# Ten of eleven groups of an up projection by Strassen's seven block products, in a decoder layer on Trainium2

## The chip, the core and the metric

The kernel runs on one core of a Trainium2 chip. The metric is the device time of one execution in microseconds, the median of several runs.

## What is computed

One decoder layer for 512 tokens of width 1024, all in fp32: a mixer of four parallel heads groups, a cross attention into 256 memory tokens, and a gated feed-forward part with a causal depthwise convolution over three tokens. The change lies in the feed-forward part:

```python
def rms_norm(t, g):
    y = t * lax.rsqrt(jnp.mean(t * t, axis=-1, keepdims=True) + RMS_EPS)
    return y * g

def conv_ffn(xn, w_up, w_conv, w_down):          # xn (512, 1024), w_up (1024, 5632), w_down (2816, 1024)
    u = causal_depthwise_conv(xn @ w_up, w_conv)  # over three tokens, each column by itself
    a, g = jnp.split(u, 2, axis=-1)
    return (a * jax.nn.silu(g)) @ w_down

h = h + conv_ffn(rms_norm(h, g_ffn), w_up, w_ffconv, w_down)
return rms_norm(h, g_final)
```

## The kernel before

Precision first. Every fp32 operand of a matmul is split into two parts of 12 bits each, hi and lo: ScalarE writes hi (a cast), VectorE lo (operand minus hi). A product is then three matmuls, hi x hi, hi x lo and lo x hi (`mm3`, L153 to L156), added up in PSUM. Weights come in loads of 512 KB, [128, 1024] values, on SyncE's DMA queue, into one of 3 raw buffers, and their parts into one of 4 buffers each (`Weights`, L97; `load_split` splits at L119 and L120). Activations are kept feature-major, [128 features, 512 tokens], as hi and lo (`Parts`, filled at L150 and L151).

The feed-forward part begins when the residual h2 is written (`Project`, L764): VectorE adds the old residual (L781), `fill` makes the parts, times the gain of the norm, ScalarE squares (L787) and GpSimd adds the squares (L788). The norm's factor per token is found after the first matmuls have begun (`h2.norm`, L792) and spread over the partitions by matmuls as `rb` [128, 512] (`row_broadcast`, L282); it is applied to what comes out of the up projection.

The up projection (L960 to L974) has 11 groups. A group is 256 columns of the a half and the same 256 of the g half, each by `pair_gemm` (L180): two output tiles [128, 512] in PSUM, 8 chunks of 128 features, three matmuls for each, so 48 matmuls of a moving operand 128x512, and 96 per group. `conv3` (L916) takes each output tile: times rb (VectorE, L918), the tap of the token itself (ScalarE, L920), and the two earlier tokens (VectorE, L921 and L922). ScalarE applies silu to g (L933) and GpSimd multiplies by a (L938 for the first ten tiles, L943 for the twelve later). The result au is split (`split_au`, L910), the first ten tiles at once, the others after the stage (L975). Between the halves of the first groups, TensorE turns the residual to token-major (`h2_tokens`, L949, copied by ScalarE at L958), and it stays in SBUF for the end.

The down projection (L1010 to L1035) is token-major: two halves of 512 output columns, four blocks of 128 tokens, 24 matmuls for each load of weights; the last block of the second half is done in two pieces of 256 columns. The final norm follows (`finish`, `scale_out`).

Each engine does its instructions in the order of the program, as a scheduler has settled it from the code's order and priorities; buffers of a pool (28 of [128, 1024] for activations, 18 of [128, 512] for others) are handed out in turn and waited for.

Of the kernel before, what the change touches and what calls it, by code (L numbers as in the profile page):

```python
# [1061 lines left out]
```

## Time and profile before

| | us |
|---|---|
| median of 3 runs | 753.76 (753.26 to 754.99) |
| span of the profiled execution | 752.2 |
| TensorE busy in it | 742.5 (99%), 3809 matmuls and transposes |
| TensorE's weight loads | 620.8 (83%), beside the matmuls |
| VectorE busy | 428.6 (57%) |
| ScalarE busy | 339.4 (45%) |
| GpSimd busy | 127.8 (17%) |

The profile is that of one execution; what the runs' clock sees and the span doesn't, 1.5 us, is about the same for each. Busy shares are means over stages. The up projection runs from about 370 to 615 us and the down projection from there to the end.

### The profile page before, as it was taken

To read this page: it belongs to the slowest core of one execution; us is meant where nothing else is said; L and a number is where in the kernel's file an instruction comes from. 1 tells how busy PE (TensorE), PEld (TensorE's weight loads), DVE (VectorE), ACT (ScalarE), POOL (GpSimd) and SP (SyncE) were. 2 spreads that over 40 slices of the span, in tenths; PEclk is the share of its full clock that TensorE was granted. 3 is DMA by queue.
4 is the path that set the end of the run, shared out by engine and by line. 5 is a ranking of instruction groups with operands and counts; after the bars stand their busy time and mean duration, and the time that the engine had idled before them with its cause. 6 is when DMAs were issued, how large, how long until landed. Compare 5 with 4: busy or idle time off the path is not lost.

```text
span 752.2 us, 9886 instructions
## 1 busy us (share of the span) xinstructions
PE 742.5 (99%) x3809; PEld 620.8 (83%) x3809; DVE 428.6 (57%) x723; ACT 339.4 (45%) x581; POOL 127.8 (17%) x140
## 2 busy tenths in 40 slices
PE   8999999999999999999999999999999999999996
PEld 7898877899988888888888888888888888888885
DVE  4868576768635436546546656666565567323214
ACT  4773654678634434444335334343333335213214
POOL 5233040033303300001211110111100114003000
PEclk9999999999999999999999999999999999999998
DMA  9743512233434422102322232232332322423202
GB/s 297 228 131 107 169 58 83 85 114 113 147 120 126 139 86 85 56 29 65 104 84 85 85 112 85 92 99 90 103 94 90 107 84 85 140 86 111 85 0 112
DMA packets 67711, 78.37 MB, mean 104 GB/s; under 512 B 3038, under 2 KB 58886, under 8 KB 67664
## 3 DMA queue, kind: packets, MB, share of 16 engines
q1 hardware_dynamic: 65040, 71.33, 30.5%
q0 software_dynamic: 2032, 5.36, 2.2%
q10 hardware_dynamic: 592, 1.05, 0.4%
q8 instruction: 30, 0.49, 0.3%
q14 instruction: 17, 0.14, 0.1%
HBM read 73.46 MB, written 4.27 MB: 103 GB/s over the span
## 4 chain that ended last, share of the span: by engine, by line
PE 98%; DMA 1%; ACT 0%; DVE 0%; issue 0%; SPq 0%; ACTq 0%
PE p_upg L154 5%; PE p_upg L156 5%; PE p_upg L155 5%; PE p_upa L154 5%; PE p_upa L155 5%; PE p_upa L156 5%; PE p_dn L154 5%; PE p_dn L156 5%; PE p_dn L155 5%; PE p_h L155 4%; PE p_h L154 4%; PE p_h L156 4%; PE p_xq L154 2%; PE p_xq L155 2%; PE p_xq L156 2%; PE p_xv L217 1%
## 5 line engine op out<-in xcount | busy, mean ns | idle before, releaser
L154 PE MATMUL p_upg<-h2g_hi,whi_upg 128*128 128x512 f32 x176 | 70.0, 398 | 0.0
L156 PE MATMUL p_upg<-h2g_hi,wlo_upg 128*128 128x512 f32 x176 | 69.5, 395 | 0.0
L155 PE MATMUL p_upg<-h2g_lo,whi_upg 128*128 128x512 f32 x176 | 69.5, 395 | 0.0
L154 PE MATMUL p_upa<-h2g_hi,whi_upa 128*128 128x512 f32 x176 | 69.2, 393 | 0.0
L155 PE MATMUL p_upa<-h2g_lo,whi_upa 128*128 128x512 f32 x176 | 68.9, 391 | 0.0
L156 PE MATMUL p_upa<-h2g_hi,wlo_upa 128*128 128x512 f32 x176 | 68.6, 390 | 0.0
L154 PE MATMUL p_dn<-whi_dn,au_hi 128*128 128x512 f32 (+1 forms) x176 | 66.7, 379 | 0.0
L156 PE MATMUL p_dn<-whi_dn,au_lo 128*128 128x512 f32 (+1 forms) x176 | 66.7, 379 | 0.0
L155 PE MATMUL p_dn<-wlo_dn,au_hi 128*128 128x512 f32 (+1 forms) x176 | 66.5, 378 | 0.0
L120 DVE TENSOR_TENSOR wlo_dn<-raw_dn,whi_dn 128x1024 fp32r<-128x1024 f32 x22 | 27.6, 1256 | 59.1 <-ACT whi_dn L119 59.0
L119 ACT CAST whi_upg<-raw_upg 128x1024 fp32r<-128x1024 f32 x22 | 23.1, 1049 | 79.3 <-PE p_upg L155 66.0
L119 ACT CAST whi_dn<-raw_dn 128x1024 fp32r<-128x1024 f32 x22 | 23.1, 1049 | 72.4 <-PE p_dn L156 30.2
L788 POOL TENSOR_TENSOR acc_h<-acc_h,sq_h 128x512 f32<-128x512 f32 x14 | 21.8, 1559 | 150.2 <-ACT sq_h L787 150.0
L943 POOL TENSOR_TENSOR au<-uo_a,sg 128x512 f32<-128x512 f32 x12 | 23.2, 1938 | 116.1 <-ACT sg L933 116.1
L120 DVE TENSOR_TENSOR wlo_upg<-raw_upg,whi_upg 128x1024 fp32r<-128x1024 f32 x22 | 27.0, 1225 | 23.2 <-ACT whi_upg L119 23.2
L156 PEld LDWEIGHTS p_upg<-h2g_hi,wlo_upg 128*128 128x128 f32 x176 | 33.1, 188 | 7.9
L154 PEld LDWEIGHTS p_upg<-h2g_hi,whi_upg 128*128 128x128 f32 x176 | 33.1, 188 | 7.7
L155 PEld LDWEIGHTS p_upg<-h2g_lo,whi_upg 128*128 128x128 f32 x176 | 33.1, 188 | 7.6
L156 PEld LDWEIGHTS p_upa<-h2g_hi,wlo_upa 128*128 128x128 f32 x176 | 33.0, 188 | 7.3
L154 PEld LDWEIGHTS p_upa<-h2g_hi,whi_upa 128*128 128x128 f32 x176 | 33.1, 188 | 7.1
L155 PEld LDWEIGHTS p_upa<-h2g_lo,whi_upa 128*128 128x128 f32 x176 | 33.1, 188 | 6.8
L156 PEld LDWEIGHTS p_dn<-whi_dn,au_lo 128*128 128x128 f32 x176 | 33.0, 188 | 6.7
(407 smaller groups left out, 1944.2 us busy)
## 6 DMA issues: line engine op xcount, KB each, us to landing
raw_upa<-in_w_up_dram SPq DMA_DIRECT2D x22, 512.0 KB, 3.6
raw_upg<-in_w_up_dram SPq DMA_DIRECT2D x22, 512.0 KB, 3.5
raw_dn<-in_w_down_dram SPq DMA_DIRECT2D x22, 512.0 KB, 3.8
raw_xk<-in_w_xkv_dram SPq DMA_DIRECT2D x8, 512.0 KB, 3.4
raw_xv<-in_w_xkv_dram SPq DMA_DIRECT2D x8, 512.0 KB, 3.6
raw_h<-in_w_out_dram SPq DMA_DIRECT2D x8, 512.0 KB, 3.5
raw_xq<-in_w_xq_dram SPq DMA_DIRECT2D x8, 512.0 KB, 3.5
raw_h<-in_w_xo_dram SPq DMA_DIRECT2D x8, 512.0 KB, 3.4
```

Of the source, the lines that this page charges most:

```text
L119: nc.scalar.copy(self.hi[:, ks], self.raw[:, ks])
L120: nc.vector.tensor_tensor(self.lo[:, ks], self.raw[:, ks], f(self.hi[:, ks]), op=ALU.subtract)
L154: nc.tensor.matmul(psum, ah, bh, start=first, stop=False, skip_group_check=True)
L155: nc.tensor.matmul(psum, ah, bl, start=False, stop=False, skip_group_check=True)
L156: nc.tensor.matmul(psum, al, bh, start=False, stop=last, skip_group_check=True)
L217: nc.tensor.matmul(p_[b], parts.hi[k][:, t], hi[:, kk, :], start=k == 0 and b % per == 0, stop=False, skip_group_check=per > 1)
L788: nc.gpsimd.tensor_tensor(acc, acc, sq, op=ALU.add)
L943: nc.gpsimd.tensor_tensor(au[i][:, j, :], ff.pop(("a", c)), sg, op=ALU.mult)
```

## The change

The first group of the up projection stays. For the other ten the product of a group is taken as one of 2 x 2 blocks: the weights as (features 0 to 511, 512 to 1023) x (256 columns of a, 256 columns of g), the activations as two halves of the features x two halves of the tokens. In place of eight products of blocks there are seven (q1 to q7, after Winograd's form), each [512 features, 256 columns] x [512 features, 256 tokens]: 4 chunks x 2 tiles x 3 matmuls = 24 matmuls of a moving operand 128x256, 168 per group. Line numbers from here on are those of the changed kernel.

- The activations' side is made once, in `operands` (L972): the residual is normed in place on VectorE (L985), GpSimd makes sums and differences (L989), and seven operands are split into parts (L981, L982; two of the lo parts on GpSimd).
- The weights' side is made per group (`Blocks`, L1011): five plain loads of 512 KB on SyncE's queue, and two of these tiles have another block of weights added to them by an adding DMA from GpSimd's queue (L1025): s3 and s1. GpSimd adds two further pairs, x11 += s1 and x12 += x11 (L1059, L1064), 128x1024 each. `product` (L1034) splits each of the seven.
- The outputs (`strassen`, L1047): al, be and ga are PSUM banks [128, 512], with the tokens' halves and tiles side by side. Products add up in al and be, and between them ScalarE copies al to SBUF (c1, c2, c3) and VectorE and ScalarE put the four output tiles ua, ug together by halves. `conv3` then works as before, without the multiplication by rb; silu is done in place.
- On TensorE the order is q1, q2, q6, q7, q5 of group 1, then q1 of group 2, q3 and q4 of group 1, q2, q6, q7 and q5 of group 2, and so on: q3 and q4 of a group stand between q1 and q2 of the next.
- All splits of au of groups 1 to 10 come after the up stage. The residual, token-major, is spilled to DRAM by GpSimd's DMAs (L963) and loaded again for the end; its transposes are moved, one half into the last part of the projection to h2, one half into group 0.
- There are 7 raw buffers instead of 3, 3 split buffers instead of 4 (for hi and lo each), 26 and 17 buffers instead of 28 and 18. In `Project` the square stands before the fill.

The core of the diff:

```diff
+ACTS, TMPS, RAWS, SPLITS = 26, 17, 7, 3
...
-    def conv3(p_, t, name):
-        u = tmp(f"u_{name}")
-        nc.vector.tensor_tensor(u, p_, ff["rb"], op=ALU.mult)
+    def conv3(u, t, name):
         o = tmp(f"uo_{name}")
...
+        def load(name, g, k, add=None):
+            t = raw_tile(f"{name}_{i}")[:, :1024]
+            v = t.rearrange("p (k n) -> p k n", n=256)
+            nc.sync.dma_start(v, src(g, k))
+            if add:
+                nc.gpsimd.dma_start(v, src(*add), accum_op=ALU.add)
+            return t
+        self.x11 = load("x11", 0, 0)
+        self.s3 = load("s3", 1, 0, (0, 0))
+        self.s1 = load("s1", 1, 0, (1, 1))
+        self.x12 = load("x12", 0, 1)
+        self.x22 = load("x22", 1, 1)
+
+    def product(psum, w, y_, name, fresh):
+        hi, lo = (t[:, :1024] for t in part_tiles(name))
+        nc.scalar.copy(hi, w)
+        nc.vector.tensor_tensor(lo, w, f(hi), op=ALU.subtract)
+        hi, lo = (t.rearrange("p (k n) -> p k n", n=256) for t in (hi, lo))
+        for k in range(4):
+            for j in range(2):
+                cs = slice(j * P, (j + 1) * P)
+                mm3(psum[:, j * 256 : j * 256 + 256], hi[:, k, cs], lo[:, k, cs], y_hi[y_][:, k, :], y_lo[y_][:, k, :], fresh and k == 0 and j == 0, k == 3)
+
+    def strassen(i):
+        w = blocks.pop(i)
+        al, be, ga = ps(f"p_al{i}"), ps(f"p_be{i}"), ps(f"p_ga{i}", "sc")
+        ua, ug = [tmp(f"ua{i}{j}") for j in range(2)], [tmp(f"ug{i}{j}") for j in range(2)]
+        product(al, w.x11, Y11, f"q1_{i}", True)
+        c1 = tmp(f"c1_{i}")
+        nc.scalar.copy(c1, al)
+        yield
+        product(ga, w.x12, Y21, f"q2_{i}", True)
+        for j, t in enumerate(tiles):
+            nc.vector.scalar_tensor_tensor(ua[j][:, :256], ga[:, t], -1.0, c1[:, t], op0=ALU.mult, op1=ALU.subtract)
+        nc.gpsimd.tensor_tensor(w.x11, w.x11, w.s1, op=ALU.add)
+        yield
+        product(al, w.x11, T2, f"q6_{i}", False)
+        c2 = tmp(f"c2_{i}")
+        nc.scalar.copy(c2, al)
+        nc.gpsimd.tensor_tensor(w.x12, w.x12, w.x11, op=ALU.add)
+        yield
+        product(be, w.s3, T3, f"q7_{i}", True)
+        yield
+        product(al, w.s1, T1, f"q5_{i}", False)
+        c3 = tmp(f"c3_{i}")
+        nc.scalar.copy(c3, al)
+        for j, t in enumerate(tiles):
+            nc.vector.tensor_tensor(ug[j][:, 256:], c3[:, t], be[:, t], op=ALU.subtract)
+        if i + 1 < NJ // 2:
+            blocks[i + 1] = Blocks(i + 1)
+        yield
+        product(al, w.x12, Y22, f"q3_{i}", False)
+        for j, t in enumerate(tiles):
+            nc.scalar.activation(ua[j][:, 256:], al[:, t], AF.Copy, scale=-1.0)
+        a = [conv3(ua[j], 2 * i + j, f"a{2 * i + j}") for j in range(2)]
+        yield
+        product(be, w.x22, T4, f"q4_{i}", False)
+        for j, t in enumerate(tiles):
+            nc.vector.tensor_tensor(ug[j][:, :256], c2[:, t], be[:, t], op=ALU.subtract)
+        for j in range(2):
+            gate(2 * i + j, a[j], ug[j])
...
+    for i in range(2, NJ // 2):
+        now = strassen(i)
+        pump(now, 1)
+        pump(before, 99)
+        pump(now, 4)
+        before = now
```

In the rows of the orders below a name is the program's, with the number of its instance behind it: whi_q7_6 is the hi part of the weights of q7 of group 6, uo_g10 the convolved g of tile 10 (group 5).

VectorE in the steady part, changed kernel, from the end of group 5's convolutions of a:

```order
L924 SCALAR_TENSOR_TENSOR uo_a11_5426<-ua51_5107,fcw_2913,uo_a11_5426 128x510
L1083 TENSOR_TENSOR ug50_5108<-c2_5_5280,p_be5_5104 128x256
L1083 TENSOR_TENSOR ug51_5109<-c2_5_5280,p_be5_5104 128x256
L1038 TENSOR_TENSOR wlo_q7_6_5536<-raw_s3_6_5345,whi_q7_6_5535 128x1024
L923 SCALAR_TENSOR_TENSOR uo_g10_5460<-ug50_5108,fcw_2913,uo_g10_5460 128x511
L923 SCALAR_TENSOR_TENSOR uo_g11_5467<-ug51_5109,fcw_2913,uo_g11_5467 128x511
L924 SCALAR_TENSOR_TENSOR uo_g10_5460<-ug50_5108,fcw_2913,uo_g10_5460 128x510
L924 SCALAR_TENSOR_TENSOR uo_g11_5467<-ug51_5109,fcw_2913,uo_g11_5467 128x510
L1058 SCALAR_TENSOR_TENSOR ua60_5358<-p_ga6_5357,c1_6_5390 128x256
L1058 SCALAR_TENSOR_TENSOR ua61_5359<-p_ga6_5357,c1_6_5390 128x256
L1038 TENSOR_TENSOR wlo_q5_6_5564<-raw_s1_6_5348,whi_q5_6_5563 128x1024
```

VectorE before, from the outputs of the g half of group 4:

```order
L918 TENSOR_TENSOR u_g8_4713<-p_upg40_4651,rb_h2_3969 128x512
L120 TENSOR_TENSOR wlo_upg5_1_4847<-raw_upg5_1_4845,whi_upg5_1_4846 128x1024
L921 SCALAR_TENSOR_TENSOR uo_g8_4715<-u_g8_4713,fcw_2913,uo_g8_4715 128x511
L922 SCALAR_TENSOR_TENSOR uo_g8_4715<-u_g8_4713,fcw_2913,uo_g8_4715 128x510
L918 TENSOR_TENSOR u_g9_4727<-p_upg41_4652,rb_h2_3969 128x512
L912 TENSOR_TENSOR au_lo4_4722<-prod8_4723,au_hi4_4721 128x512
L921 SCALAR_TENSOR_TENSOR uo_g9_4729<-u_g9_4727,fcw_2913,uo_g9_4729 128x511
L922 SCALAR_TENSOR_TENSOR uo_g9_4729<-u_g9_4727,fcw_2913,uo_g9_4729 128x510
L120 TENSOR_TENSOR wlo_upa6_0_4898<-raw_upa6_0_4896,whi_upa6_0_4897 128x1024
L912 TENSOR_TENSOR au_lo4_4722<-prod9_4735,au_hi4_4721 128x512
L918 TENSOR_TENSOR u_a10_4801<-p_upa50_4739,rb_h2_3969 128x512
```

Where a group had two operations on each PSUM tile and four weight parts, the conv steps and assemblies of group 5 now stand between the weight parts of q7 and q5 of group 6, which TensorE takes up next.

GpSimd at the entry of the stage, changed kernel (h12 and h13 hold the features 512 to 1023 of the residual; ylo2 and ylo6 are the lo parts of Y22 and T4; the L1025 row is an adding DMA):

```order
L1064 TENSOR_TENSOR raw_x12_1_4014<-raw_x12_1_4014,raw_x11_1_4006 128x1024
L989 TENSOR_TENSOR h12_2588<-h12_2588,h10_2586 128x2x256
L989 TENSOR_TENSOR h13_2589<-h13_2589,h11_2587 128x2x256
L982 TENSOR_TENSOR ylo2_4027<-h12_2588,yhi2_4026 128x512
L982 TENSOR_TENSOR ylo2_4027<-h13_2589,yhi2_4026 128x512
L982 TENSOR_TENSOR ylo6_4035<-h12_2588,yhi6_4034 128x512
L982 TENSOR_TENSOR ylo6_4035<-h13_2589,yhi6_4034 128x512
L1025 DMA raw_s1_2_4340<-in_w_up_dram 128x4x256
L1059 TENSOR_TENSOR raw_x11_2_4335<-raw_x11_2_4335,raw_s1_2_4340 128x1024
L936 TENSOR_TENSOR prod0_4290<-uo_a0_4216,uo_g0_4283 128x512
L1064 TENSOR_TENSOR raw_x12_2_4343<-raw_x12_2_4343,raw_x11_2_4335 128x1024
```

GpSimd before, at the same place:

```order
L788 TENSOR_TENSOR acc_h2_3433<-acc_h2_3433,sq_h24_3763 128x512
L788 TENSOR_TENSOR acc_h2_3433<-acc_h2_3433,sq_h25_3769 128x512
L788 TENSOR_TENSOR acc_h2_3433<-acc_h2_3433,sq_h26_3837 128x512
L788 TENSOR_TENSOR acc_h2_3433<-acc_h2_3433,sq_h27_3843 128x512
L938 TENSOR_TENSOR prod0_4036<-uo_a0_3973,sg0_4032 128x512
L938 TENSOR_TENSOR prod1_4048<-uo_a1_3979,sg1_4046 128x512
```

The product of tile 0 (prod0) followed the sums of squares at once; now it stands behind operand work, an adding DMA and an add for group 2.

ScalarE in the changed kernel, at the first q6 (yhi2 and yhi6 are the hi parts of Y22 and T4):

```order
L1037 CAST whi_q6_1_4220<-raw_x11_1_4006 128x1024
L981 CAST yhi2_4026<-h12_2588 128x512
L981 CAST yhi2_4026<-h13_2589 128x512
L981 CAST yhi6_4034<-h12_2588 128x512
L981 CAST yhi6_4034<-h13_2589 128x512
L1054 COPY c1_1_4183<-p_al1_4148 128x512
L1037 CAST whi_q7_1_4251<-raw_s3_1_4008 128x1024
```

and some rows later, before q2 of group 2:

```order
L1037 CAST whi_q3_1_4384<-raw_x12_1_4014 128x1024
L931 ACT_TABLE_LOAD
L931 ACTIVATE uo_g0_4283<-uo_g0_4283 128x512
L1037 CAST whi_q4_1_4422<-raw_x22_1_4016 128x1024
L914 CAST au_hi0_4288<-prod0_4290 128x512
L922 ACTIVATE uo_g1_4294<-u_11_4146,fcw_2913 128x512
L1037 CAST whi_q2_2_4465<-raw_x12_2_4343 128x1024
```

ScalarE before, after the factor rb:

```order
L119 CAST whi_upg1_1_4172<-raw_upg1_1_4171 128x1024
L958 COPY h2t0_3983<-pt_h01_4020 128x512
L920 ACTIVATE uo_g0_4028<-u_g0_4026,fcw_2913 128x512
L933 ACT_TABLE_LOAD
L933 ACTIVATE sg0_4032<-uo_g0_4028 128x512
L119 CAST whi_upa2_0_4230<-raw_upa2_0_4229 128x1024
L911 CAST au_hi0_4034<-prod0_4036 128x512
L920 ACTIVATE uo_g1_4042<-u_g1_4040,fcw_2913 128x512
```

The copy c1 and the split of group 2's q2 now stand behind casts that wait for GpSimd (yhi6 and au_hi0).

## Rows read from the trace of the kernel before

**Rows 1.** The page: its head, and busy time and transfers of the whole kernel.

```profile
span 752.2 us, 9886 instructions
...
PE 742.5 (99%) x3809; PEld 620.8 (83%) x3809; DVE 428.6 (57%) x723; ACT 339.4 (45%) x581; POOL 127.8 (17%) x140
...
GB/s 297 228 131 107 169 58 83 85 114 113 147 120 126 139 86 85 56 29 65 104 84 85 85 112 85 92 99 90 103 94 90 107 84 85 140 86 111 85 0 112
```

**Rows 2.** Windows: one up group long, in the middle of the stage.

```profile
core 0: us, PE busy (x) PEld busy (x) DVE busy (x) ACT busy (x) POOL busy (x), PEclk, DMA share, GB/s
...
518.00:540.30 22.30, 22.30 (x98) 18.19 (x97) 13.69 (x17) 8.12 (x11) 2.93 (x3) 1.00 0.31 94
```

**Rows 3.** The chain of waits (start, us, engine, output, line), two groups apart.

```profile
479.40 0.24 PE p_upg L154
...
501.54 0.24 PE p_upg L154
```

**Rows 4.** Timeline: 256-wide matmuls and a weight load (PEld) of the down projection.

```profile
741.23 0.28 PE L154 MATMUL p_dn<-whi_dn,au_hi 128*128 128x256 f32 x1
...
745.36 0.28 PE L156 MATMUL p_dn1last<-whi_dn,au_lo 128*128 128x256 f32 x1
...
741.23 0.19 PEld L155 LDWEIGHTS p_dn<-wlo_dn,au_hi 128*128 128x128 f32 x1
```

**Rows 5.** Timeline of VectorE in the up stage.

```profile
505.01 1.41 DVE L921 SCALAR_TENSOR_TENSOR uo_a<-u_a,fcw,uo_a 128x511 f32<-128x511 f32 x2
...
513.61 1.23 DVE L120 TENSOR_TENSOR wlo_upg<-raw_upg,whi_upg 128x1024 fp32r<-128x1024 f32 x1 [0.85 <-ACT whi_upg L119]
514.75 0.75 DVE L921 SCALAR_TENSOR_TENSOR uo_g<-u_g,fcw,uo_g 128x511 f32<-128x511 f32 x1
```

**Rows 6.** Groups by line and form, VectorE, from 370 us: a 256-wide operation on PSUM.

```profile
L988 DVE TENSOR_TENSOR h2t<-p_dn,h2t 128x256 f32<-128x256 f32 x1 | 0.4, 419 | 0.0
```

**Rows 7.** Timeline of GpSimd, alone at 45.68 and beside VectorE.

```profile
45.68 1.03 POOL L449 TENSOR_TENSOR rb<-rb_x 128x512 f32<-128x512 f32 x1 [9.06 <-ACT rb_x L290]
...
352.83 1.39 POOL L788 TENSOR_TENSOR acc_h<-acc_h,sq_h 128x512 f32<-128x512 f32 x1 [88.49 <-ACT sq_h L787]
355.07 3.17 POOL L788 TENSOR_TENSOR acc_h<-acc_h,sq_h 128x512 f32<-128x512 f32 x2 [0.86 <-ACT sq_h L787]
```

**Rows 8.** Timeline of VectorE at the same time.

```profile
351.65 1.41 DVE L151 SCALAR_TENSOR_TENSOR h2g_lo<-h,vec,h2g_hi 128x512 fp32r<-128x512 f32 x2
352.97 1.28 DVE L781 TENSOR_TENSOR h<-p_h,h 128x512 f32<-128x512 f32 x2
...
355.30 3.49 DVE L151 SCALAR_TENSOR_TENSOR h2g_lo<-h,vec,h2g_hi 128x512 fp32r<-128x512 f32 x2
```

**Rows 9.** Groups by line and form, ScalarE, from 340 us.

```profile
L119 ACT CAST whi_upg<-raw_upg 128x1024 fp32r<-128x1024 f32 x22 | 23.1, 1049 | 79.3 <-PE p_upg L155 66.0 <-issue 8.8 <-PE p_h L155 4.5
...
L920 ACT ACTIVATE uo_g<-u_g,fcw 128x512 f32<-128x512 f32 x22 | 15.8, 718 | 0.0
...
L911 ACT CAST au_hi<-prod 128x512 fp32r<-128x512 f32 x10 | 6.2, 621 | 13.6 <-POOL prod L938 13.6
```

**Rows 10.** Groups by line and form, GpSimd: the product, and issuing a DMA.

```profile
L943 POOL TENSOR_TENSOR au<-uo_a,sg 128x512 f32<-128x512 f32 x12 | 23.2, 1938 | 116.1 <-ACT sg L933 116.1
...
L780 POOL DMA_DIRECT2D old_h<-xT x8 | 4.4, 558 | 3.2 <-PE psc_f L685 3.2
```

**Rows 11.** DMA issues (times, KB each, median us from issue to landing).

```profile
raw_upg<-in_w_up_dram SPq DMA_DIRECT2D x22, 512.0 KB, 3.5
...
gfin<-in_g_final_dram POOLq DMA_DIRECT2D x1, 512.0 KB, 4.8
```

**Rows 12.** Timeline of TensorE after an idle stretch (in brackets).

```profile
6.89 1.12 PE L354 MATMUL pt_x<-ident,x_cols 128*128 128x128 f32 x4 [1.51 <-DMA x_cols<-in_x_dram]
...
9.94 0.63 PE L156 MATMUL p_hc<-xg_hi,wlo_hc 128*128 128x512 f32 x1
10.37 0.62 PE L155 MATMUL p_hc<-xg_lo,whi_hc 128*128 128x512 f32 x1
```

More of the change, by code (lines that the diff above doesn't have):

```diff
@@ L94, in f, with raw_tile, part_tiles @@
         return t.bitcast(F32)
+    def raw_tile(name):
+        return wp.tile([P, 1040], F32, tag="raw", name=f"raw_{name}", bufs=RAWS)
+    def part_tiles(name):
+        return (wp.tile([P, 1040], F32R, tag=tag, name=f"{tag}_{name}", bufs=SPLITS) for tag in ("whi", "wlo"))
     class Weights:
@@ L767, in __init__ @@
             if spilled is not None:
-                res = [act4(f"{name}{i}") for i in range(4)]
-                res = [res[c // 2][:, c % 2, :] for c in range(KC)]
+                self.tiles = [act4(f"{name}{i}") for i in range(4)]
+                res = [self.tiles[c // 2][:, c % 2, :] for c in range(KC)]
             self.h = res
@@ L781, in done @@
                     nc.vector.tensor_tensor(res[c], p_, old, op=ALU.add)
-                    self.hg.fill(c, res[c], g[:, c : c + 1])
                     if c == 0:
@@ L896, in trunk @@
     xvalues(3)
-    for g in h2.pairs:
+    for g in h2.pairs[:3]:
         pump(g, 99)
-    SPLIT_EARLY = 10
-    au = {}
-    au_hi, au_lo = {}, {}
+    au, au_hi, au_lo = {}, {}, {}
     def split_tiles(i):
@@ new lines, in trunk @@
+    blocks = {}
+    def strassen(i):
[36 more added lines that the diff above has]
+            gate(2 * i + j, a[j], ug[j])
@@ new lines, in trunk @@
+    gneg = cp.tile([P, KC], F32, name="gneg")
+    nc.vector.tensor_scalar(gneg, vg["ffn"], -1.0, None, op0=ALU.mult)
+    pump(h2.pairs[3], 2)
+    for b in range(NB):
+        h2_tokens(2 * b)
+    pump(h2.pairs[3], 99)
+    ga = pair_gemm(Wu[:, 0:256], h2.hg, "upa", first_done(0))
+    gg = pair_gemm(Wu[:, DFF : DFF + 256], h2.hg, "upg", first_done(1))
+    pump(ga, 2)
+    r2 = h2.norm()
+    pump(ga, 1)
+    ff["rb"] = row_broadcast(r2, "h2", "po")
+    pump(ga, 1)
+    for b in range(NB):
+        h2_tokens(2 * b + 1)
@@ new lines, in trunk @@
+    blocks[1] = Blocks(1)
+    pump(ga, 99)
+    operands()
+    pump(gg, 99)
+    before = strassen(1)
+    first_a = []
+    for j in range(2):
+        pump(before, 2)
+        first_a.append(conv3(first_u[0, j], j, f"a{j}"))
+    for j in range(2):
+        gate(j, first_a[j], first_u[1, j])
+    pump(before, 1)
+    for i in range(2, NJ // 2):
[4 more added lines that the diff above has]
+        before = now
+    pump(before, 99)
+    for i in range(1, NJ // 2):
@@ L984, in trunk @@
     v0 = cp.tile([P, 4], F32, name="v0")
+    h2t = []
+    for b in range(NB):
+        h2t.append(flat(act4(f"h2t{b}")))
+        nc.sync.dma_start(h2t[b], h2s[b])
     def finish(b, half, c0, c1):
```

110 lines of the change are left out of this document (67 added, 43 removed).

## The prediction

> **What bounds the kernel now.** First the head of the page: TensorE is busy 742.5 of 752.2 us [rows 1], so a change gains only by taking work off TensorE, and loses wherever TensorE waits. Next the table of windows for a stretch as long as one up group, in the middle of that stage: 22.30 of 22.30 us busy at a granted clock of 1.00 (2.4 GHz), VectorE 13.69, ScalarE 8.12, GpSimd 2.93 [rows 2]. So VectorE has 8.6 us of slack per group there, ScalarE 14. Third the chain of waits: the same matmul of the g half comes round every 501.54 - 479.40 = 22.14 us [rows 3]; that is one group of 96 matmuls 128x512, 0.2306 us each.
>
> The profiled span is 752.2 us, the median of the runs 753.76: I sum against the span and add 1.5. A measurement here can tell 0.2%, about 1.5 us.
>
> **1. TensorE's work: -23.2.** A group becomes seven products of 24 matmuls, each 128x256: 168 instead of 96. Does half the width cost half the time? The last block of the down projection has such matmuls, each with its own weight load: 35 steps from 741.23 to 745.36, 4.13 / 35 = 0.118 us [rows 4]. The weight loads there read 0.19 us but do not set the pace. 168 x 0.118 = 19.82; ten groups gain 10 x (22.14 - 19.82) = 23.2. The break-even pitch would be 22.14 / 168 = 0.132. All other matmuls keep their number.
>
> **2. The loop of VectorE, ScalarE and GpSimd in the steady part: +9.6 (0 to +17).** Per group the change doubles what VectorE does to weights. Prices, as pitches in the DVE timeline: a lo part 128x1024, 1.14 (513.61 to 514.75); a conv step 0.66 (two in 1.33, 505.01 to 506.33) [rows 5]; a 256-wide operation with a PSUM operand, 0.42 as listed [rows 6], about 0.35 as a pitch. Seven lo parts 8.0, eight conv steps 5.3, six short ones 2.1: 15.4 us. GpSimd has two products at 1.03, as such an operation takes alone at 45.68 [rows 7], and two adds of twice that size, 2.06 each: 6.2.
>
> These don't simply lie side by side. At 355 us two GpSimd adds and two VectorE operations, both with two SBUF inputs, run together and take 3.17 and 3.49 us; alone they take 2 x 1.03 and 1.41 [rows 7, 8]: 2.06 + 1.41 = 3.47, as if one after the other. At 352.97 two VectorE operations whose one input is PSUM take 1.28 beside a GpSimd add, no more than alone [rows 7, 8]. So 8.0 + 5.3 + 6.2 = 19.5 exclude one another, and the 2.1 may overlap GpSimd: VectorE's round is between 19.5 and 21.6, against TensorE's 19.82. The Trainium skill ("SBUF — State Buffer", section "Who interferes with whom") says that a VectorE instruction with at most one SBUF input does not contend with GpSimd, and one with two does, for the whole instruction; the rows agree, and by it the floor is the 19.5, where without it one would count 15.4.
>
> The order has a loop too. There are three split buffers, so q6 of group i+1 takes the one that q3 of group i frees. From the end of q3 VectorE does, in the order shown: whi of q6 1.05 (ScalarE) with ua 0.7 and a conv copy 0.72 [rows 9], four conv steps 2.64, ug 0.7, lo of q7 1.14, four gate steps 2.64, ua 0.7, lo of q5 1.14: 11.4 us. Then q5, q1 and q3 follow on TensorE, 3 x 2.83 = 8.5, and the loop closes at 19.9, just over TensorE's 19.82. One excluded GpSimd product makes it 21.0. I take 21.0, the middle of the 19.5 to 21.6: 1.2 above TensorE, over 8 rounds 9.6. Ends: 0 (all of GpSimd falls in gaps), 17 (21.9). ScalarE has 7 casts at 1.05, 4 conv copies at 0.72, 2 silu at about 0.62 and some 2.4 of copies, 13.9: hidden.
>
> **3. First use of the operands, q6 of group 1: +9 (0 to +13).** TensorE gets there 57 matmuls 128x512 (13.1), four blocks of transposes (1.4) and two products (5.7) after rb: 20.2. Until then VectorE has eight norm steps, ten lo halves (18 x 0.66 = 11.9) and three weight lo parts (3.4): 15.3. GpSimd has, ahead of the last y21 add, two weight adds (4.1) and eight combines (8.2): 12.3. One after the other 27.6. ScalarE's copy c1, which q6 waits for, stands behind the casts of T4, which wait for y21: 1.3 more, 28.9. Nothing covers this: TensorE has no other work in its order. Low end: the two chains overlap where they wait for each other's data.
>
> **4. q2 of group 2: +3.5 (0 to +9).** On ScalarE the split of group 0's product stands ahead of whi of q2. That product stands on GpSimd behind the add x11 += s1, which waits for the adding DMA, and that is issued behind the lo halves of Y22 and T4 (both orders are shown). From the start of q6 of group 1: four such halves, 4.1, with VectorE's weight parts between them about 6; issue 0.56 [rows 10]; the adding DMA A; the add 2.06 and 1 of exclusion; product 1.3; ScalarE 0.62, 0.72 and 1.05; lo part 1.14: 14.4 + A. TensorE has six products till then, 17.0. No row has an adding DMA. Nearest: 512 KB on GpSimd's queue in 4.8, and twice the plain load's 3.5, 7.0, if the destination is read and written [rows 11]. I take A = 6, so 20.4 against 17.0; ends A = 3 and 12. The Trainium skill ("DMA: Bandwidth & Descriptors", "Anatomy of one DMA") gives 2.0 us plus bytes / 436e3 per us for a GpSimd DMA, an estimate of 3.2 here, and by it this term would be 0.6; no run here shows it.
>
> **5. Leaving the stage: +3.5 (0 to +5).** The split of the first down weights waits for a buffer as q4's (1.05). On ScalarE the last silu and group 1's second au split (0.62 each, as for au_hi [rows 9]) stand with the early down splits; their order makes the second down group late. The 20 deferred au splits cost ScalarE and VectorE 1.2 and 1.4 per down group of 5.5 us: hidden.
>
> **6. Slow matmuls after idling: +1 (0 to +3).** After 1.51 us of idling, 512-wide matmuls come every 0.43 us (9.94 to 10.37), against 0.23 in the stage [rows 12]; each wait of several microseconds may cost some such matmuls.
>
> **Nothing for:** the raw buffers (7, from 3) and split buffers (3, from 4) ahead of the up stage (-1 to +3: with two in use the third is split during 2.8 to 5.5 us of matmuls, splits take 2.2); the residual's way through DRAM, which has the whole stage; DMA load, seven transfers of 512 KB per 20 us, some 185 GB/s, where the first slices of the page move 297 and 228 [rows 1]. The multiplication by rb is gone from VectorE for ten groups, counted in the lists above.
>
> Sum: 752.2 - 23.2 + 9.6 + 9 + 3.5 + 3.5 + 1 = 755.6; runs **757**.
>
> **Rivals.** *A, the other side:* VectorE's and GpSimd's work interleave without stretching the loop: a round stays at 19.82. It decides at a loop below 19.9, that is if GpSimd's 6.2 us fall into VectorE's waits. For it: 19.5 is under 19.82, and VectorE does wait for TensorE at several places. Against it: no slack at all, and the product in this stage reads 1.94 on average instead of 1.03 [rows 10]. Time: without term 2, and with terms 3 to 6 between a quarter of my 17 and all of it, span 752.2 - 23.2 + (4 to 17) = 733 to 746, runs 735 to 747.5, middle about 742. Chance 0.32.
>
> *B, the adding DMA is slow.* s1 of group i+1 takes the buffer of x11 of group i. Load 3.5, issue 0.6, A, two adds 4.1 and the split 1.7 make a loop of 9.9 + A. It binds above A = 10 and reaches the old 22.14 at A = 12.3; at A = 14 a round is 23.9, ten rounds cost 41, and the span is 752.2 - 23.2 + 41 + 17 = 787, the runs 789. For it: nothing shows such a DMA. Against it: that is four times the plain load. Chance 0.09.
>
> *C, the 256-wide matmuls run slower than at the end of the kernel,* above 0.132: then the gain is gone and terms 3 to 6 remain, 752.2 + 17, the runs 771. For it: weight loads read 0.19 [rows 4]; against: the same rows. Chance 0.03. That the change doesn't do what it says: the order has 1680 matmuls 128x256 in the stage; nothing.
>
> **Numbers.** The forecast has 0.56, with its own range 749 to 770; A 0.32, B 0.09, C 0.03. The range 740 to 774 leaves out the lower part of A (0.11) and nearly all of B (0.08). Faster than 752.3: A and a little of the forecast (0.02), 0.34. Within 0.2%, from the forecast alone: 0.08. Slower than 755.3: the rest, 0.58.
>
> **What would show it.** Right: TensorE in the stage busy about 19.8 of 21 us per group, its waits ended by VectorE's lo of q5 and of q6; GpSimd's adds read well over 2.06; idle stretches of 9 and 3.5 us before q6 of group 1 and q2 of group 2. Wrong: rounds at 19.8 (A), waits ended by DMAs (B), a pitch other than 0.118 (C), or an idle stretch at a place that I gave nothing.

## The result and the profile after

The changed kernel takes 797.16 us, median of 4 runs (786.25 to 802.04), against 753.77: ratio 1.0529, 95% interval 1.0458 to 1.0599. The forecast was 757, range 740 to 774. Slower was the likeliest side; the size is far outside. Ratios here and below are of the executions in the faster of two states: the one of 802.04 is not in this one, nor one of 1828.24 in that of experiment 3.

The page of the changed kernel, busy times and the granted clock in 40 slices (PE is TensorE, PEld its weight loads, DVE VectorE, ACT ScalarE, POOL GpSimd, SP SyncE):

```profile
span 795.7 us, 11708 instructions
...
PE 741.6 (93%) x4529; PEld 652.0 (82%) x4529; DVE 517.6 (65%) x792; ACT 396.0 (50%) x675; POOL 231.6 (29%) x200
...
PEclk9999999999999999999987898899999999999999
```

Against [rows 1] TensorE idles 54.1 us (795.7 - 741.6) where it idled 9.7. It is as busy as before, though it should have 23.2 us less to do: 719.3, so 22.3 us of its busy time are extra. The account, -23.2 + 44.4 + 22.3 = 43.5, closes on the difference of the spans by construction, since the 22.3 are what is left over. In the stretches of the stage in which the clock was granted at 0.50, TensorE is busy for 30.8 us; at 0.21 us for a matmul instead of 0.118 these cost some 14 us. The other 8 are not accounted for.

The longest waits of TensorE from 390 to 680 us (us in total, times, longest):

```profile
PE p_al L161 <- DVE wlo_q L1038: 20.1, 6, 6.0
PE p_al L159 <- ACT c L1063: 6.3, 5, 2.3
PE p_al L159 <- ACT c L1054: 5.2, 1, 5.2
PE p_ga L159 <- ACT whi_q L1037: 5.0, 1, 5.0
PE p_be L161 <- DVE wlo_q L1038: 3.1, 3, 1.0
PE p_dn L159 <- ACT au_hi L914: 2.3, 1, 2.3
```

No wait is ended by a DMA; most by VectorE's lo parts of the weights. The timeline of TensorE gives their places (start of the first matmul after the wait; wait and releaser in brackets):

```profile
414.49 0.58 PE L159 MATMUL p_al<-yhi,whi_q 128*128 128x256 f32 x1 [5.17 <-ACT c L1054]
421.26 0.58 PE L161 MATMUL p_al<-yhi,wlo_q 128*128 128x256 f32 x1 [5.98 <-DVE wlo_q L1038]
440.20 0.58 PE L159 MATMUL p_ga<-yhi,whi_q 128*128 128x256 f32 x1 [5.00 <-ACT whi_q L1037]
459.38 0.38 PE L159 MATMUL p_al<-yhi,whi_q 128*128 128x256 f32 x1 [2.31 <-ACT c L1063]
480.32 0.39 PE L159 MATMUL p_al<-yhi,whi_q 128*128 128x256 f32 x1 [0.99 <-ACT c L1063]
484.15 0.58 PE L161 MATMUL p_al<-yhi,wlo_q 128*128 128x256 f32 x1 [3.33 <-DVE wlo_q L1038]
509.91 0.58 PE L161 MATMUL p_al<-yhi,wlo_q 128*128 128x256 f32 x1 [3.40 <-DVE wlo_q L1038]
536.24 0.49 PE L161 MATMUL p_al<-yhi,wlo_q 128*128 128x256 f32 x1 [3.28 <-DVE wlo_q L1038]
...
650.74 0.38 PE L159 MATMUL p_al<-yhi,whi_q 128*128 128x256 f32 x1 [1.01 <-ACT c L1063]
```

The first two stand ahead of and in q6 of group 1, the third is q2 of group 2. 459.38 and 650.74 are the starts of q5 of groups 2 and 10: eight rounds of (650.74 - 459.38) / 8 = 23.92 us, where the forecast had 21.0 and TensorE needs 19.82. In that window it is busy 170.37 us, so 21.0 are waits, and 170.37 - 8 x 19.82 = 11.8 are extra busy time. The rounds are not alike: four take 25.2 to 26.5 us, three 22.6 or 22.7 and the first 20.9.

What holds up lo of q5 (the wait of 3.33) is seen on VectorE:

```profile
475.21 1.22 DVE L1038 TENSOR_TENSOR wlo_q<-raw_s,whi_q 128x1024 fp32r<-128x1024 f32 x1
...
479.66 4.44 DVE L1038 TENSOR_TENSOR wlo_q<-raw_s,whi_q 128x1024 fp32r<-128x1024 f32 x1
```

and on GpSimd at the same time:

```profile
479.23 1.27 POOL L1025 DMA_DIRECT2D raw_s<-in_w_up_dram  x1 [7.10 <-PE p_be L160]
480.00 3.01 POOL L941 TENSOR_TENSOR au<-uo_a,uo_g 128x512 f32<-128x512 f32 x2
485.50 3.11 POOL L1059 TENSOR_TENSOR raw_x<-raw_x,raw_s 128x1024 f32<-128x1024 f32 x1 [2.49 <-DVE wlo_q L1038]
```

The subtraction that takes 1.2 us for q7 (475.21) takes 4.44 for q5: its own 1.14 and both GpSimd products, 3.01, which began 0.34 us after it (0.34 + 3.01 + 1.14 = 4.49). At 505.35 the same comes again (4.51, beside products of 3.00); four of the eight lo parts of q5 from group 3 on read 4.4 to 4.5, the others 1.2 or 1.9. The products come so late because the issue of an adding DMA, 1.27 us long, stands ahead of them in GpSimd's queue (experiments 2 and 3).

Windows of the changed kernel (busy time of PE, PEld, DVE, ACT and POOL, then the granted clock, the DMA engines' share and GB/s) show what follows such a wait:

```profile
484.00:488.60 4.60, 4.45 (x21) 4.45 (x22) 2.37 (x3) 0.00 (x0) 3.10 (x1) 0.50 0.80 204
488.60:509.90 21.30, 17.80 (x149) 17.39 (x148) 17.32 (x20) 12.90 (x18) 7.41 (x6) 0.98 0.60 132
```

After 3.33 us of idling the clock is granted at 0.50, the 1.2 GHz level, until about 488.6, and twenty matmuls come 0.21 us apart, not 0.118.

### The profile page after: what moved, and what is told of

Its sections match the earlier page's. It is cut to its first block, busy times and chain, and to the rows that moved or that the text cites. A ratio compares the mean times of both kernels' runs of the same rounds, so it can differ in the third digit from the quotient of the medians.

```text
span 795.7 us, 11708 instructions
## 1 busy us (share of the span) xinstructions
PE 741.6 (93%) x4529; PEld 652.0 (82%) x4529; DVE 517.6 (65%) x792; ACT 396.0 (50%) x675; POOL 231.6 (29%) x200
## 5 line engine op out<-in xcount | busy, mean ns | idle before, releaser
L161 PE MATMUL p_al<-yhi,wlo_q 128*128 128x256 f32 x320 | 95.8, 300 | 20.4 <-DVE wlo_q L1038 20.1
L1038 DVE TENSOR_TENSOR wlo_q<-raw_x,whi_q 128x1024 fp32r<-128x1024 f32 x50 | 75.5, 1523 | 49.9 <-ACT whi_q L1037 49.9
L159 PE MATMUL p_al<-yhi,whi_q 128*128 128x256 f32 x320 | 96.3, 301 | 11.8 <-ACT c L1063 6.3
L160 PE MATMUL p_al<-ylo,whi_q 128*128 128x256 f32 x320 | 95.0, 297 | 0.0
L1037 ACT CAST whi_q<-raw_x 128x1024 fp32r<-128x1024 f32 x50 | 52.4, 1048 | 82.9 <-PE p_al L160 60.1
L161 PEld LDWEIGHTS p_al<-yhi,wlo_q 128*128 128x128 f32 x320 | 66.0, 206 | 22.3 <-DVE wlo_q L1038 22.3
L159 PEld LDWEIGHTS p_al<-yhi,whi_q 128*128 128x128 f32 x320 | 66.1, 207 | 13.9 <-ACT c L1063 8.5
L1025 POOL DMA_DIRECT2D raw_s<-in_w_up_dram x20 | 25.7, 1286 | 150.4 <-DMA raw_s<-in_w_up_dram 95.0
L160 PEld LDWEIGHTS p_al<-ylo,whi_q 128*128 128x128 f32 x320 | 65.8, 206 | 0.1
L124 ACT CAST whi_dn<-raw_dn 128x1024 fp32r<-128x1024 f32 x22 | 23.1, 1049 | 73.6 <-PE p_dn L161 33.3
L161 PE MATMUL p_be<-yhi,wlo_q 128*128 128x256 f32 x160 | 45.2, 282 | 3.1 <-DVE wlo_q L1038 3.1
L941 POOL TENSOR_TENSOR au<-uo_a,uo_g 128x512 f32<-128x512 f32 x20 | 38.0, 2018 | 30.8 <-ACT uo_g L931 30.8
L159 PE MATMUL p_be<-yhi,whi_q 128*128 128x256 f32 x160 | 45.2, 282 | 0.0
```

Source lines behind the costliest of these rows:

```text
L124: nc.scalar.copy(self.hi[:, ks], self.raw[:, ks])
L159: nc.tensor.matmul(psum, ah, bh, start=first, stop=False, skip_group_check=True)
L160: nc.tensor.matmul(psum, ah, bl, start=False, stop=False, skip_group_check=True)
L161: nc.tensor.matmul(psum, al, bh, start=False, stop=last, skip_group_check=True)
L941: nc.gpsimd.tensor_tensor(au[i][:, j, :], a, sg, op=ALU.mult)
L1025: nc.gpsimd.dma_start(v, src(*add), accum_op=ALU.add)
```

## The experiments

After this profile, theory **P**: what GpSimd does with two SBUF inputs keeps VectorE out, and the forecast counted too little of it. **Q**: the adding DMA is what comes late. **Q'**, formed after the second run: not its duration but the place of its issue in GpSimd's queue. A "round" is the distance of the starts of ScalarE's copy c2 from group to group, averaged over the eight that end at groups 3 to 10 (changed kernel 23.92).

**1. No products on GpSimd.** Silu writes au itself; the multiplication by a is left out.

```diff
-            nc.gpsimd.tensor_tensor(au[i][:, j, :], a, sg, op=ALU.mult)
+            nc.scalar.activation(au[i][:, j, :], sg, AF.Silu)
```

> Leaves out the GpSimd products of groups 1 to 10 (silu writes au directly, a is not multiplied in). Theory P: the two products stand beside the lo part of q5 and keep VectorE from it (4.45 us in place of 1.14), TensorE idles 3.3 us and then runs slowly for some 4 us. Without them the lo part of q5 reads 1.2 in every round, the waits of 3.3 go, and with five such rounds of 3.3 + 2.2 the time is 765 to 772. Theory Q: the rounds are set by load, adding DMA, GpSimd add and q6; then rounds of 22 to 24 us stay and the time is 785 or more.

775.44 (772.97 to 776.51), ratio 1.0289 [1.0258, 1.0320], 3 us above P's range; round 21.37. The waits of 3.3 us are gone. What stays are GpSimd's two adds, each keeping a lo part back. VectorE and GpSimd in this run:

```profile
505.45 3.47 DVE L1038 TENSOR_TENSOR wlo_q<-raw_x,whi_q 128x1024 fp32r<-128x1024 f32 x1 [1.73 <-ACT whi_q L1037]
...
511.13 3.21 DVE L1038 TENSOR_TENSOR wlo_q<-raw_x,whi_q 128x1024 fp32r<-128x1024 f32 x1 [0.41 <-ACT whi_q L1037]
```

```profile
505.45 2.39 POOL L1059 TENSOR_TENSOR raw_x<-raw_x,raw_s 128x1024 f32<-128x1024 f32 x1 [4.61 <-issue]
510.85 2.40 POOL L1064 TENSOR_TENSOR raw_x<-raw_x,raw_x 128x1024 f32<-128x1024 f32 x1 [3.01 <-DVE wlo_q L1038]
```

3.47 is 2.39 + 1.14 within 0.1. So the products are 2.5 us of the 4.1 per round. The same run answers another reading of the 4.44, that the issue of the adding DMA itself keeps VectorE out: here lo of q5 runs beside such an issue and takes 1.22.

```profile
499.55 1.29 POOL L1025 DMA_DIRECT2D raw_s<-in_w_up_dram  x1 [6.85 <-DVE uo_g L924]
...
500.23 1.22 DVE L1038 TENSOR_TENSOR wlo_q<-raw_s,whi_q 128x1024 fp32r<-128x1024 f32 x1
```

**2. No adding DMAs.** The blocks that they would add are left out of s3 and s1.

```diff
-                if add:
-                    nc.gpsimd.dma_start(v, src(*add), accum_op=ALU.add)
```

> Leaves out the adding DMAs (s3 and s1 hold one block of weights each instead of a sum). Theory Q: rounds fall to 20 to 21 us, the time to 765 or less. Theory P: the products still stand beside the lo part of q5, rounds of about 25.8 us stay, the time is 785 to 800.

783.82 (782.07 to 784.81), 1.0402 [1.0373, 1.0431]; round 21.98, between the two expectations. The products still meet lo of q5, but begin 0.44 us ahead of it (504.16 against 504.60), and it takes 1.93 us, not 4.4:

```profile
504.60 1.93 DVE L1036 TENSOR_TENSOR wlo_q<-raw_s,whi_q 128x1024 fp32r<-128x1024 f32 x1
506.45 2.31 DVE L1036 TENSOR_TENSOR wlo_q<-raw_x,whi_q 128x1024 fp32r<-128x1024 f32 x1
```

```profile
504.16 1.29 POOL L941 TENSOR_TENSOR au<-uo_a,uo_g 128x512 f32<-128x512 f32 x1 [8.31 <-ACT uo_g L931]
...
505.42 2.27 POOL L941 TENSOR_TENSOR au<-uo_a,uo_g 128x512 f32<-128x512 f32 x1
```

lo of q5 gets in between the two products: it waits for the first only, the second product waits for it, and the next lo part (2.31) waits for the second product. VectorE loses about as much, but more than half of it on a piece that TensorE needs later. P and Q are both in it: the products shut VectorE out, the DMA's issue decides when.

**3. s1 loaded, and added to, first** of the five blocks: all DMAs stay, and the issue that stood ahead of the products is out of their way.

```diff
+        self.s1 = load("s1", 1, 0, (1, 1))
         self.x11 = load("x11", 0, 0)
         self.s3 = load("s3", 1, 0, (0, 0))
-        self.s1 = load("s1", 1, 0, (1, 1))
```

> s1 is loaded (and added to) ahead of x11 and s3, so that its buffer is one freed a group earlier, not x11's of the group before; the result is unchanged. Theory Q': the products are late, and so beside the lo part of q5, since on GpSimd's queue they stand behind the issue of the adding DMA of s1, which waits for the load of its buffer. Then it goes as without adding DMAs: rounds of 22 us, about 784. If the products meet the lo part of q5 anyway (silu sets their time), 793 to 800.

785.33 (783.10 to 785.35), 1.0418 [1.0395, 1.0442]; round 22.27. With every adding DMA in place this is 1.5 us above the run without them: Q', not the DMA's duration.

**4. Products later:** behind the add x11 += s1 of the next group but one.

```diff
         nc.gpsimd.tensor_tensor(w.x11, w.x11, w.s1, op=ALU.add)
+        products(i - 2)
```

> Each group's two products stand behind the add x11 += s1 of the group after the next on GpSimd's queue, not ahead of it; the result is unchanged. Theory P: the lo part of q5 is free of them, where VectorE now idles they cost little: 765 to 775. Theory Q: the rounds keep their length, 790 to 800.

789.22 (788.22 to 791.38), 1.0480 [1.0451, 1.0510]; round 22.75. A miss: the time is nearly Q's, though lo of q5 is back at 1.2 us. The products now keep back a step of the convolution of a. VectorE, groups by line and form, 459 to 651 us:

```profile
L923 DVE SCALAR_TENSOR_TENSOR uo_a<-ua,fcw,uo_a 128x511 f32<-128x511 f32 x16 | 28.4, 1812 | 0.0
L923 DVE SCALAR_TENSOR_TENSOR uo_g<-ug,fcw,uo_g 128x511 f32<-128x511 f32 x18 | 12.6, 740 | 0.0
```

The same step takes 1812 ns for a and 740 for g. Moving GpSimd's work only chooses who is kept back.

**5. No GpSimd in the loop at all:** products, both adds and the adding DMAs are left out, the edits of 1 and 2 and

```diff
-        nc.gpsimd.tensor_tensor(w.x11, w.x11, w.s1, op=ALU.add)
...
-        nc.gpsimd.tensor_tensor(w.x12, w.x12, w.x11, op=ALU.add)
```

> Leaves out all that GpSimd does per group in the steady part: the adds x11 += s1 and x12 += x11, the products (silu writes au) and the adding DMAs. Theory P (whatever GpSimd does beside VectorE's chain from q3's end to the lo part of q5 lengthens the round, and slow matmuls follow each long wait): rounds are VectorE's own loop, 19.9 us or TensorE's 19.8, no waits of over 0.5 us in them; eight rounds of 23.9 become 20, -31, and the entry loses the weight adds, some -6: about 760. Rival V: VectorE's own chain with the steps between engines is longer than 19.9, rounds of 21 and more stay, 768 or more.

755.21 (753.24 to 758.19), 1.0026 [1.0011, 1.0041]; round 19.90. TensorE does not idle once in the loop, at a clock of 0.99:

```profile
454.18:613.42 159.24, 159.24 (x1342) 159.24 (x1343) 124.20 (x168) 101.64 (x143) 0.00 (x0) 0.99 0.42 133
```

So GpSimd's part of the loop is what makes 23.92 out of 19.9: 4.0 us per round. This run doesn't yet tell the work from the place where it is done; the next run does.

**6. The same sums and products on VectorE,** for groups 1 to 10. Nothing is left out; the adding DMAs stay on GpSimd's queue.

```diff
-            nc.gpsimd.tensor_tensor(au[i][:, j, :], a, sg, op=ALU.mult)
+            nc.vector.tensor_tensor(au[i][:, j, :], a, sg, op=ALU.mult)
...
-        nc.gpsimd.tensor_tensor(w.x11, w.x11, w.s1, op=ALU.add)
+        nc.vector.tensor_tensor(w.x11, w.x11, w.s1, op=ALU.add)
...
-        nc.gpsimd.tensor_tensor(w.x12, w.x12, w.x11, op=ALU.add)
+        nc.vector.tensor_tensor(w.x12, w.x12, w.x11, op=ALU.add)
```

> The two adds of weight blocks and the two products of a group are VectorE's instead of GpSimd's; the result is unchanged. Theory P: GpSimd's operations cost VectorE 2.4 and 1.5 us each by exclusion, its own 1.14 and 0.66: VectorE has 15.4 + 2.3 + 1.3 = 19.0 us of work per round, rounds of 20 to 21, time 770 to 777. Rival: VectorE is full, more work on it makes it worse: rounds of 24 and more, 797 or above.

761.74 (759.17 to 763.02), 1.0121 [1.0101, 1.0140], better than expected; round 19.96. A window of the loop, and two operations of VectorE:

```profile
459.00:612.00 153.00, 151.91 (x1287) 151.30 (x1286) 144.66 (x193) 98.42 (x139) 17.96 (x14) 1.00 0.74 180
```

```profile
493.23 1.29 DVE L941 TENSOR_TENSOR au<-uo_a,uo_g 128x512 f32<-128x512 f32 x2
...
496.70 1.22 DVE L1059 TENSOR_TENSOR raw_x<-raw_x,raw_s 128x1024 f32<-128x1024 f32 x1
```

VectorE is busy 95% of the time (144.66 of 153.00), and TensorE idles there for 1.1 us in all. Two products cost VectorE 1.29 us there, where GpSimd's kept it out for 3.0; an add 1.2 instead of 2.4. With the adding DMAs in place and the round at 19.96, it is not their traffic that made the rounds long, nor a VectorE with too much to do. What stays are the waits at the entry, somewhat shorter (4.13, 4.87, 2.06, 1.90 and 2.31 us).

**7. TensorE kept busy:** useless matmuls (93, 46, and 28 per round) where it waited, in the kernel of the change.

```diff
+        for _ in range(n):
+            nc.tensor.matmul(warm[0][:, :256], y_hi[0][:, 0, :128], y_hi[0][:, 1, :], start=True, stop=True, skip_group_check=True)
```

> Adds matmuls of no use on a spare PSUM bank where TensorE waits: 93 ahead of q6 of group 1, 46 ahead of q2 of group 2, 28 ahead of each q5 from group 3 on; the result is unchanged. Theory R: of the 43 us lost, some 22 are matmuls at half speed after a wait. Then the pitch stays at 0.118 and the time falls by 15 to 22, to 775 to 782. If slow matmuls have another cause, the time is 797 or, by useless work where there was no wait, up to 10 longer.

793.62 (792.99 to 794.17), 1.0536 [1.0505, 1.0568]: a miss against the expected 775 to 782. The granted clock is 0.997 over the span, but 28 such matmuls are 3.3 us, so that a round cannot be under 19.8 + 3.3 = 23.1, and it is 23.15. The edit pays for the clock with what the clock gives back.

**8. The same at the entry alone,** on run 6.

```diff
+        keep_busy(32 if i == 2 else 0)
...
+        keep_busy(74 if i == 1 else 0)
```

> The run with sums and products on VectorE, with matmuls of no use on a spare PSUM bank where TensorE still waits at the entry: 74 ahead of q6 of group 1, 32 ahead of q2 of group 2; the result is unchanged. In that run TensorE is busy all through the later rounds, so time lost at the entry is not taken up by a later wait. Theory R (a wait of several microseconds costs its length again in part, by matmuls at the granted 0.50): the stretches at 0.50 after both waits, some 4 to 5 us of loss by the windows, go: 762 becomes 757 to 759. If slow matmuls cost nothing, 762; if the useless matmuls only shift the wait, 762 to 764.

759.72 (757.29 to 764.61), 1.0074 [1.0051, 1.0098], against 1.0121 [1.0101, 1.0140] of run 6, with intervals that all but touch; 757 to 759 was expected. Slow matmuls at the entry cost some 2 us, if anything. That what they lose is mostly taken off the next wait is likely, but not shown.

**9. Two plain groups** ahead of the first Strassen group instead of one, to give the operands time, in the kernel of the change.

```diff
-    before = strassen(1)
+    ga = pair_gemm(Wu[:, 256:512], h2.hg, "upa1", first_done(1, 0))
+    gg = pair_gemm(Wu[:, DFF + 256 : DFF + 512], h2.hg, "upg1", first_done(1, 1))
...
+    before = strassen(2)
```

> Group 1 is done as group 0, by 96 matmuls 128x512, and nine groups by seven products; the result is unchanged. The operands have 22 us more of TensorE's work as cover: the waits of 0.8 + 11.2 us before q2 and q6 of the first group and the slow matmuls behind them (2 to 3) go, 2.3 us of work comes back and one round of 23.9 becomes one of 22.1: -13 to -16, about 782. If what is late there is not the operands but the loads or the adding DMA, -5 or less.

796.13 (793.03 to 801.43), 1.0579 [1.0525, 1.0632]: a miss, about 782 was expected. The work on the operands now keeps VectorE from emptying the plain group's PSUM, and the wait for c1 is still there:

```profile
416.85 0.47 PE L159 MATMUL p_upg<-h2g_hi,whi_upg 128*128 128x512 f32 x1 [3.16 <-DVE u L948]
...
451.03 0.58 PE L159 MATMUL p_al<-yhi,whi_q 128*128 128x256 f32 x1 [4.96 <-ACT c L1054]
```

**10. The operands on VectorE too,** in the order in which the block products need them, the weights' parts of q1 and q2 ahead; on run 6. The gate products of group 0 go to VectorE as well, and the au of group 1 is split at once.

```diff
-                nc.gpsimd.tensor_tensor(out[m], x[m], y_[m], op=op)
+                nc.vector.tensor_tensor(out[m], x[m], y_[m], op=op)
...
-        split(Y22, y22, nc.gpsimd)
-        split(T4, y21, nc.gpsimd)
+        split(Y22, y22)
+        split(T4, y21)
```

> The run with sums and products on VectorE, and in addition: the operands' sums and the lo parts of Y22 and T4 on VectorE, made in the order in which TensorE needs them (Y11, Y21, T2 before q6; T3, T1 then; Y22 and T4 last), q1 and q2 split ahead of T2; the first two groups' au split at once. The result is unchanged. Theory P for the entry: GpSimd's eight sums and four lo parts cost VectorE 1.6 us each by exclusion, its own 0.66. VectorE then is done with q6's data some 22 us after rb, TensorE arrives at 20: the waits of 9 and 4 us there fall to 2 to 4 in all, the exit's 4 to 1 or 2: 752.2 - 23.2 + 3 to 8, runs 733 to 739, faster than before. Rival: the entry is bound by the loads, the adding DMA or ScalarE's order: 750 or more.

761.96 (757.45 to 766.23), 1.0117 [1.0086, 1.0148]: a miss in time (733 to 739 was expected), and the theory's first half right. q6 of group 1 is reached with waits of under 0.7 us each, where run 6 had 9.0 in two and the changed kernel 12; but two others have grown, ahead of q5 of groups 1 and 2:

```profile
424.47 0.58 PE L161 MATMUL p_al<-yhi,wlo_q 128*128 128x256 f32 x1 [5.62 <-DVE wlo_q L1042]
...
460.34 0.58 PE L159 MATMUL p_al<-yhi,whi_q 128*128 128x256 f32 x1 [8.53 <-ACT c L1072]
```

The first stands behind group 0's convolutions in VectorE's order; the second behind an add that waits for the adding DMA of s1.

**11. Both put in order,** on run 10: s1 first (the edit of 3), those convolutions behind lo of q5, group 0's gate later, and the au splits of groups 1 and 2 moved into the middle of the stage.

```diff
+    first_a = [conv3(first_u[0, j], j, f"a{j}") for j in range(2)]
...
+        if i == 2:
+            for j in range(2):
+                gate(j, first_a[j], first_u[1, j])
...
+        if i in (6, 7):
+            split_tiles(i - 5)
+            for j in range(2):
+                split_au(2 * (i - 5) + j, au[i - 5][:, j, :])
```

> The run with the entry on VectorE, in which the waits had moved on: 5.6 us before q5 of group 1 (VectorE convolves group 0 ahead of its lo part) and 8.5 us before q5 of group 3 (VectorE's add x11 += s1 waits for the adding DMA of s1, and ScalarE's copy c2 for what stands behind it). Here s1 is loaded and added to first, as in that earlier run, group 0's convolutions come behind q5, and the au splits of groups 1 and 2 stand in the middle of the stage; the result is unchanged. Theory: both waits go, what stays is group 0's 8 us of VectorE, for which its rounds have only 0.8 us each to spare, so some 6 us of waits: 752.2 - 23.2 + 6 + 2 to 8 more, runs 738 to 747, faster than before. Rival: the waits move again to the next late piece and the time stays at 755 to 762.

749.06 (746.71 to 749.65), 0.9940 [0.9923, 0.9956]: 0.6% faster than the kernel before, and just above the expected 738 to 747. What each of the edits is worth isn't told apart. One long wait is left, 4.64 us before q5 of group 2: ScalarE's copy c2 stands behind a silu of group 1.

**12. That copy first:**

```diff
+        yield
...
+        if i == 2:
+            pump(before, 2)
+            pump(now, 2)
+            pump(before, 99)
+            pump(now, 2)
```

> As the kernel of the run before (749.06), with one thing in another order: ScalarE's copy of c2 of group 2 stands ahead of group 1's gate conversions and silus. Theory (what is left of the entry is one late copy in ScalarE's in-order queue): the wait of 4.64 us ahead of q5 of group 2 falls to 1 to 2, the matmuls behind it stay at a pitch of 0.12, and the time falls to 743 to 747. Rival (the wait moves to the next in line, VectorE's conversions, which now get their input later): a wait of 2 to 4 us shows up at one of the next products and the time stays at 748 to 750.

**746.43** (745.74 to 747.37), **0.9902** [0.9884, 0.9919], the fastest: 6.4% under the changed kernel, 1.0% under the kernel before. The expected 743 to 747 holds, and the rival has its share: the 4.64 fell to 1.55, and a wait of 1.62 appeared a little later. Waits of TensorE, 400 to 620 us:

```profile
PE p_al L161 <- DVE wlo_q L1042: 3.9, 5, 1.7
PE p_al L159 <- ACT c L1072: 2.1, 2, 1.5
PE p_al L159 <- ACT c L1079: 1.6, 1, 1.6
PE p_ga L159 <- ACT whi_q L1041: 1.0, 1, 1.0
PE p_dn L159 <- ACT whi_dn L124: 1.0, 1, 1.0
```

## Why the prediction was right or wrong

**Right: term 1, TensorE's work.** After the slow matmuls of 484 us the 256-wide ones come 0.118 us apart, and without GpSimd a round is 19.90, forecast 19.82. Rival C is out. The 23.2 us are there to be had.

Added up as measured, the terms give -23.2 + 32.8 (loop) + 12.0 + 5.5 + 2.3 + 3.9 + 10.5 (the extra busy time outside the loop) = 43.8, against 43.5; the 32.8 hold 21.0 of waits and 11.8 of the 22.3 of extra busy time.

**Wrong: term 2, the loop: +9.6 taken, its end at 17, 32.8 measured** (8 x (23.92 - 19.82)). The mechanism was named: GpSimd's and VectorE's work with two SBUF inputs exclude one another. The step that failed is "one excluded GpSimd product makes it 21.0": in the long rounds both fall on lo of q5, and the two adds each fall on another lo part that TensorE waits for (run 1). That step took it that GpSimd's operations could lie anywhere in the round, and left out the issue of the adding DMA in GpSimd's queue, which sends the products to the worst place (runs 2 and 3: 1.7 to 1.9 us per round). It added up work, 19.5 to 21.6, as if VectorE had to be full; in the 191.36 us of the loop it was idle for 43.7, and TensorE waited all the same, for the one lo part that was held up. The short first round, 20.9, is the only one near the 21.0.

The prices were low as well. A product was put at 1.03, an add at 2.06; alone they take 1.29 (run 2) and 2.4, and with their own waits for VectorE 1.99 on average, and 3.06 for x11 += s1. The row at 45.68 behind the 1.03 multiplies a tile by itself (rb<-rb_x). The trace of the kernel before had the price for two different tiles, which is higher:

```profile
L938 POOL TENSOR_TENSOR prod<-uo_a,sg 128x512 f32<-128x512 f32 x10 | 13.4, 1341 | 107.8 <-ACT sg L933 83.4 <-PE p_upa L155 24.4
```

At 1.29 and 2.4 the work that excludes one another is 20.7 us, not 19.5: above TensorE's 19.82 from the start. GpSimd is busy for 11.0 us per round (87.77 / 8), its two issues among them; the forecast had 6.2 without issues. The middle of 19.5 and 21.6 is 20.55, not 21.0; with it the term would have been 5.8.

Runs 5 and 6 are the proof: without GpSimd, or with the same work on VectorE, the loop goes at TensorE's pace. The sentence of the Trainium skill that the prediction used ("SBUF — State Buffer", "Who interferes with whom") is borne out by the pairs shown here, 3.47 = 2.39 + 1.14 best of all; what the forecast lacked was the conclusion that an operation is then cheaper on VectorE itself.

**Term 3, the entry: right place, 9 taken, 12.0 measured** (0.82 + 5.17 + 5.98), within its range. The same exclusion: the lo halves and sums take 1.7 us each on average on both engines, 0.68 when VectorE has all of them (run 10).

**Term 4, q2 of group 2: 3.5 taken, 5.5 measured.** The length of the chain came out near, 18.9 us from 421.3 to 440.2 against a forecast of 20.4 with A taken as 6, but partly by luck. The four lo halves that it put at 6 were done at 420.0. In their place stood a step that it left out, the plain load into the same tile, which starts when lo of q6 is done and x11's buffer is free:

```profile
421.27 0.37 SPq L1023 DMA_DIRECT2D raw_s<-in_w_up_dram  x1
...
425.34 1.33 POOL L1025 DMA_DIRECT2D raw_s<-in_w_up_dram  x1 [5.33 <-DVE uo_a L923]
433.35 2.39 POOL L1059 TENSOR_TENSOR raw_x<-raw_x,raw_s 128x1024 f32<-128x1024 f32 x1 [6.68 <-DMA raw_s<-in_w_up_dram]
```

That is 4.1 us, then 7.9 for the adding DMA with its issue and 7.0 to the start of q2. The cover was wrong: four products stand ahead of q2 of group 2 on TensorE from the start of q6, not six: 11.3 us at full pace, 13.9 as they ran, with slow matmuls among them. The window up to the wait has 94 matmuls (four products are 96, and two of q6 had run before):

```profile
421.26:435.20 13.94, 13.93 (x94) 13.73 (x94) 10.41 (x13) 6.68 (x8) 3.18 (x2) 0.79 0.73 187
```

Here q3 and q4 of group 1 come behind q2 of group 2, other than in the later groups and than the description of the change has it. A cover shorter by 3.1 us and a chain shorter by 1.5 partly cancelled. Another 2.31 us came before q5 of group 2, a place that the forecast had at nothing.

**Term 5, leaving the stage: right,** 3.5 taken, 3.9 measured (1.01 + 2.27 + 0.57).

**Term 6, slow matmuls: +1 taken, some 14 measured in the stretches at 0.50,** of the 22.3 us of extra busy time. The row was right (0.43 for 0.23 after idling [rows 12]) and the number of such stretches was not: there are seven in the stage. How much of this the end of the kernel sees stays open: run 7 bought it back and lost it again, run 8 found some 2 us at the entry. In the loop another wait for VectorE follows anyway.

**Rival A,** rounds at 19.82, came with runs 5 and 6, not with the change: GpSimd's work doesn't fall into VectorE's waits. **Rival B** named the adding DMA and was wrong in its mechanism: the loop of 9.9 + A is 17.2 us with the measured 7.3, below the round, and no wait of TensorE is ended by it directly. Its chain of buffer, load and adding DMA does show at the entry (term 4, and the wait of 8.53 us in run 10). The range was too narrow because terms 2 and 6 were given ends of 17 and 3.

## What to carry to other kernels

Work moved to GpSimd to relieve VectorE doesn't relieve it where both have two SBUF inputs: count it as VectorE's time at GpSimd's pace, and see first whether VectorE can do it itself (here 753.6 became 746.4 that way, once the order was right too, and 797 the other). For each instruction that is moved to a queue, look at what it waits for and what stands behind it there; the place of an issue of 1.3 us was worth 1.7 us per round. Each wait that was taken away showed the next one; go on along the order, one at a time, until the sum is paid.
